# RMSNorm with each row written twice: rows spread in place to eight output rows in one buffer, one 64 KB run per partition and store, all transfers issued by SyncE

## Chip, cores, metric

One core of a Trainium2 chip, the other cores idle. The metric is the device time of one execution in microseconds (us). Most executions of the kernel before agree within 0.2%. A run more than 1.5% above the fastest of its kernel is called slow and left out of every comparison. "MB" is a million bytes. "Kilobytes" of a row or a packet are 1024 bytes.

## The reference

Every row of x is repeated, divided by its root mean square and multiplied by gamma.

```python
B, S, D = 8, 512, 2048                      # x: float32, 4096 rows of 8 KB
x_rep = np.repeat(x, 2, axis=1)             # each row twice, one after the other
rms = np.sqrt((x_rep ** 2).mean(axis=-1, keepdims=True) + 1e-6)
return (x_rep / rms) * gamma[None, None, :] # 8192 rows of 8 KB
```

The kernel must read 33.55 MB and write 67.11 MB. The two copies of a row are neighbours in memory, so the results of k neighbouring rows fill one run of 2k x 8 KB.

## The kernel before

Two rows per partition, 16 tiles, six buffers for x and six for the result. Each tile is loaded by SyncE in one transfer and stored by GpSimd in two, one for each copy.

```python
K = 2
x_t = x_f.rearrange("(n p k) d -> n p k d", p=P, k=K)
out_t = out_v.rearrange("(n p k) r d -> n p k r d", p=P, k=K)
BUFS = 6
# ... pools, gamma: loaded by SyncE, then copied to all partitions by GpSimd ...
for i in range(ntiles):
    x_tile = xin.tile([P, K, D], mybir.dt.float32, name="x_tile")
    nc.sync.dma_start(out=x_tile[:], in_=x_t[i])
    sq_tile = sq.tile([P, K, D], mybir.dt.float32, name="sq_tile")
    # ... ScalarE: Square of each row into sq_tile with the sum in ss; Sqrt; VectorE: reciprocal ...
    y_tile = sq_tile
    for k in range(K):
        nc.vector.tensor_scalar_mul(
            out=y_tile[:, k, :], in0=x_tile[:, k, :], scalar1=rstd[:, k : k + 1])
    nc.vector.tensor_mul(out=y_tile[:], in0=y_tile[:], in1=gamma_kd)
    for r in range(R):
        nc.gpsimd.dma_start(out=out_t[i, :, :, r, :], in_=y_tile[:])
```

Of the kernel before, what the change touches and what calls it, by code (L numbers as in the profile page):

```python
# [1 line left out]

# [4 lines left out]


@with_exitstack  # L10
def kernel(
    ctx: ExitStack,
    tc: tile.TileContext,
    x: bass.AP,
    gamma: bass.AP,
    out: bass.AP,
):
    nc = tc.nc
    P = nc.NUM_PARTITIONS

    B, S, D = x.shape
    Bo, So, Do = out.shape
    R = So // S
    assert D == Do and B == Bo and So == S * R
    eps = 1e-6

    x_f = x.rearrange("b s d -> (b s) d")
    N = B * S
    K = 2
    assert N % (P * K) == 0  # L30
    ntiles = N // (P * K)
    x_t = x_f.rearrange("(n p k) d -> n p k d", p=P, k=K)

    out_v = out.rearrange("b (s r) d -> (b s) r d", r=R)
    out_t = out_v.rearrange("(n p k) r d -> n p k r d", p=P, k=K)

    BUFS = 6
    singles = ctx.enter_context(tc.tile_pool(name="singles", bufs=1))
    xin = ctx.enter_context(tc.tile_pool(name="xin", bufs=BUFS))
    sq = ctx.enter_context(tc.tile_pool(name="sq", bufs=BUFS))  # L40
    small = ctx.enter_context(tc.tile_pool(name="small", bufs=8))

    gamma_b = singles.tile([P, D], mybir.dt.float32)
    nc.sync.dma_start(out=gamma_b[0:1, :], in_=gamma.partition_broadcast(1))
    nc.gpsimd.partition_broadcast(out_ap=gamma_b[:], in_ap=gamma_b[0:1, :])  # L45
    gamma_kd = bass.AP(
        tensor=gamma_b.tensor,
        offset=gamma_b.offset,
        ap=[gamma_b.ap[0], [0, K], gamma_b.ap[1]],
    )  # L50

    eps_t = singles.tile([P, 1], mybir.dt.float32)
    nc.vector.memset(eps_t, eps)  # L53

    inv_d = 1.0 / float(D)

    for i in range(ntiles):
        x_tile = xin.tile([P, K, D], mybir.dt.float32, name="x_tile")
        nc.sync.dma_start(out=x_tile[:], in_=x_t[i])

        sq_tile = sq.tile([P, K, D], mybir.dt.float32, name="sq_tile")
        ss = small.tile([P, K], mybir.dt.float32, name="ss")
        for k in range(K):
            nc.scalar.activation(  # L64
                out=sq_tile[:, k, :],
                in_=x_tile[:, k, :],
                func=mybir.ActivationFunctionType.Square,
                accum_out=ss[:, k : k + 1],
            )

        rms = small.tile([P, K], mybir.dt.float32, name="rms")
        nc.scalar.activation(  # L72
            out=rms[:],
            in_=ss[:],
            func=mybir.ActivationFunctionType.Sqrt,
            scale=inv_d,
            bias=eps_t[:],
        )
        rstd = small.tile([P, K], mybir.dt.float32, name="rstd")
        nc.vector.reciprocal(out=rstd[:], in_=rms[:])  # L80

        y_tile = sq_tile
        for k in range(K):
            nc.vector.tensor_scalar_mul(  # L84
                out=y_tile[:, k, :], in0=x_tile[:, k, :], scalar1=rstd[:, k : k + 1]
            )
        nc.vector.tensor_mul(out=y_tile[:], in0=y_tile[:], in1=gamma_kd)  # L87

        for r in range(R):
            nc.gpsimd.dma_start(out=out_t[i, :, :, r, :], in_=y_tile[:])  # L90


# [1 line left out]
_INS = ['x', 'gamma']  # L94
_OUTS = [((8, 1024, 2048), 'float32')]


# [23 lines left out]
```

## Time and profile before

| | before |
|---|---|
| time, median | 245.0 us |
| span of the profiled run | 243.0 us |
| DMA engines full (16 busy) until | 238.7 us |
| last engine moves its last byte at | 240.6 us |

The two lower rows come from the records of single DMA packets in the trace. They list start, duration, size and queue of each packet, but not its engine; "full" means that 16 packets are open at once. The remaining 2.5 us of the span are completion and the end of the program.

The page of the kernel before: busy time by engine, then the DMA engines in 40 slices of 6.1 us (a 9 means 90% or more), and the packets of each queue.

```profile
span 243.0 us, 320 instructions
DVE 112.7 (46%) x65; ACT 69.5 (29%) x82; POOL 30.2 (12%) x37
...
DMA  6999999999999999999999999999999999999993
GB/s 222 431 431 431 391 433 429 436 417 442 422 431 430 433 422 431 429 427 430 425 430 450 410 426 426 430 425 430 429 425 418 418 417 419 430 417 425 417 426 160
...
q0 software_dynamic: 8704, 67.11, 65.7%
q1 hardware_dynamic: 2306, 33.56, 32.8%
```

No compute engine is busy for half of the span, and the DMA engines are full from the second slice to the last but one. So the kernel is bound by its transfers: time can come only from the rate while the engines are full, from the two edges, or from gaps. q0 is GpSimd's queue: 8192 packets of 8 KB and 512 completions. q1 is SyncE's: 2048 packets of 16 KB.

Windows of the same trace (microseconds from the start; columns are busy time of VectorE, ScalarE and GpSimd with instruction counts, the TensorE clock, the DMA share and the rate). A packet is counted where it starts, so short windows are coarse.

```profile
core 0: us, DVE busy (x) ACT busy (x) POOL busy (x), PEclk, DMA share, GB/s
30.00:130.00 100.00, 54.38 (x31) 28.19 (x33) 14.70 (x16) 1.00 1.01 430
140.00:170.00 30.00, 18.89 (x12) 12.57 (x15) 4.09 (x6) 1.00 1.01 428
175.00:200.00 25.00, 14.45 (x8) 4.24 (x6) 3.40 (x5) 1.00 1.01 422
200.00:235.00 35.00, 0.00 (x0) 0.00 (x0) 0.68 (x1) 1.00 1.01 421
```

From 140 us on there are only stores. They begin at 428 GB/s and drop to 421 after 175 us, with the engines full throughout: a packet that took 309 ns takes about 314.

The two costliest compute groups (line, engine, operation, shapes, count | busy us, mean ns | idle before, and what ended it):

```profile
L64 ACT ACTIVATE sq_tile<-x_tile 128x2048 f32<-128x2048 f32 x32 | 60.8, 1901 | 114.1 <-DMA out_dram<-sq_tile 101.1
L87 DVE TENSOR_TENSOR sq_tile<-sq_tile,gamma_b 128x4096 f32<-128x4096 f32 x16 | 70.8, 4422 | 0.5
```

ScalarE stood idle for 114 us, 101 of them until a store had landed and freed a buffer. Compute waits for DMA, not the reverse.

### The profile page before, as it was taken

The numbers are of one execution on the slowest core, as the hardware profiler recorded it, in microseconds if no ns is written. First come the engines' busy times: TensorE is split into PE (matmuls) and PEld (weight loads), VectorE is DVE, ScalarE is ACT, GpSimd is POOL, SyncE is SP. The second block draws the span as 40 slices with busy tenths as digits, with TensorE's granted clock in tenths as the row PEclk, the third lists the DMA queues.
The fourth block names the chain that finished last, engine by engine and source line by source line (L and its number), as shares of the span: only waits on it lengthen the run. The fifth ranks groups of instructions, "written<-read, shape, count | busy, mean of one in ns | idle before, by whom it ended". The sixth has DMA issues, their size and how long they took to land.

```text
span 243.0 us, 320 instructions
## 1 busy us (share of the span) xinstructions
DVE 112.7 (46%) x65; ACT 69.5 (29%) x82; POOL 30.2 (12%) x37
## 2 busy tenths in 40 slices
DVE  0069999950900049680095709577595600000000
ACT  2598656006000150600615061541624000000000
POOL 4003223411010101110130111111121111000000
DMA  6999999999999999999999999999999999999993
GB/s 222 431 431 431 391 433 429 436 417 442 422 431 430 433 422 431 429 427 430 425 430 450 410 426 426 430 425 430 429 425 418 418 417 419 430 417 425 417 426 160
DMA packets 11012, 100.69 MB, mean 414 GB/s; under 512 B 769, under 2 KB 769, under 8 KB 769
## 3 DMA queue, kind: packets, MB, share of 16 engines
q0 software_dynamic: 8704, 67.11, 65.7%
q1 hardware_dynamic: 2306, 33.56, 32.8%
q14 instruction: 2, 0.02, 0.0%
HBM read 33.56 MB, written 67.11 MB: 414 GB/s over the span
## 4 chain that ended last, share of the span: by engine, by line
DMA 50%; another core or an unknown queue 15%; issue 4%; ACT 3%; DVE 2%; POOL 1%; POOLq 0%; ACTq 0%
DMA out_dram<-sq_tile 50%; ACT sq_tile L64 3%; DVE sq_tile L87 2%; POOL out_dram L90 1%; POOLq L116 0%; ACT rms L72 0%; DVE rstd L80 0%; ACTq L64 0%; POOLq L90 0%
## 5 line engine op out<-in xcount | busy, mean ns | idle before, releaser
L64 ACT ACTIVATE sq_tile<-x_tile 128x2048 f32<-128x2048 f32 x32 | 60.8, 1901 | 114.1 <-DMA out_dram<-sq_tile 101.1
L87 DVE TENSOR_TENSOR sq_tile<-sq_tile,gamma_b 128x4096 f32<-128x4096 f32 x16 | 70.8, 4422 | 0.5
L90 POOL DMA_DIRECT2D out_dram<-sq_tile x32 | 27.7, 867 | 169.3 <-DMA out_dram<-sq_tile 125.6
L84 DVE TENSOR_SCALAR sq_tile<-x_tile,rstd 128x2048 f32<-128x2048 f32 x32 | 40.2, 1298 | 0.5
L80 DVE RECIPROCAL rstd<-rms 128x2 f32<-128x2 f32 x16 | 2.6, 163 | 77.8 <-ACT rms L72 77.8
L64 ACT ACTIVATION_READ_ACCUMULATOR sq_tile<-x_tile 128x1 f32 x32 | 6.0, 186 | 0.0
L72 ACT ACTIVATE rms<-ss,eps_t 128x2 f32<-128x2 f32 x16 | 4.7, 296 | 0.5
L45 POOL PARTITION_BROADCAST gamma_b<-gamma_b x1 | 2.3, 2293 | 2.1 <-DMA gamma_b<-in_gamma_dram 2.1
L64 ACT ACT_TABLE_LOAD x1 | 1.3, 1283 | 0.7 <-PEq L105 0.7
L72 ACT ACT_TABLE_LOAD x1 | 1.3, 1283 | 0.0
L53 DVE MEMSET eps_t<- 128x1 f32 x1 | 0.1, 59 | 0.8 <-PEq L105 0.8
L105 POOL MEMSET const-float32-0.0<- 128x1 f32 x1 | 0.1, 99 | 0.2 <-issue 0.2
L105 POOL MEMSET const-uint8-127<- 128x1 uint8 x1 | 0.1, 103 | 0.0
L105 POOL MEMSET const-bfloat16-1.0<- 128x1 bf16 x1 | 0.1, 102 | 0.0
L105 POOL MEMSET const-float32-1.0<- 128x1 f32 x1 | 0.1, 99 | 0.0
## 6 DMA issues: line engine op xcount, KB each, us to landing
out_dram<-sq_tile POOLq DMA_DIRECT2D x32, 2048.0 KB, 40.7
x_tile<-in_x_dram SPq DMA_DIRECT2D x16, 2048.0 KB, 24.4
gamma_b<-in_gamma_dram SPq DMA_DIRECT2D x1, 8.0 KB
```

What stands on the lines that cost most here:

```text
L45: nc.gpsimd.partition_broadcast(out_ap=gamma_b[:], in_ap=gamma_b[0:1, :])
L53: nc.vector.memset(eps_t, eps)
L64: nc.scalar.activation(out=sq_tile[:, k, :], in_=x_tile[:, k, :], func=mybir.ActivationFunctionType.Square, accum_out=ss[:, k : k + 1],)
L72: nc.scalar.activation(out=rms[:], in_=ss[:], func=mybir.ActivationFunctionType.Sqrt, scale=inv_d, bias=eps_t[:],)
L80: nc.vector.reciprocal(out=rstd[:], in_=rms[:])
L84: nc.vector.tensor_scalar_mul(out=y_tile[:, k, :], in0=x_tile[:, k, :], scalar1=rstd[:, k : k + 1])
L87: nc.vector.tensor_mul(out=y_tile[:], in0=y_tile[:], in1=gamma_kd)
L90: nc.gpsimd.dma_start(out=out_t[i, :, :, r, :], in_=y_tile[:])
L105: nc = _bacc.Bacc("TRN2", target_bir_lowering=False, num_devices=1)
```

## The change

Intent: fewer and longer packets, one queue, no store work on GpSimd. A buffer of 64 KB per partition holds eight output rows. Four rows of x are loaded into its upper half; row after row is normalized into its place and copied to the row beside it (three copies on ScalarE, one on VectorE). The whole buffer is then one store, one run of 64 KB per partition. There are three such buffers and eight tiles; SyncE issues loads and stores. Scale and gamma are fused in one VectorE instruction, and squares go to PSUM, a memory apart from the buffers that the transfers use.

```diff
-    K = 2
+    K = 4
-    xin = ctx.enter_context(tc.tile_pool(name="xin", bufs=BUFS))
-    sq = ctx.enter_context(tc.tile_pool(name="sq", bufs=BUFS))
+    rows = ctx.enter_context(tc.tile_pool(name="rows", bufs=3))
+    junk = ctx.enter_context(tc.tile_pool(name="junk", bufs=1, space=bass.MemoryType.PSUM))
+    def load(i, parts=1):
+        y = rows.tile([P, K * R, D], f32, name="y")
+        step = K // parts
+        for k in range(0, K, step):
+            at = K * (R - 1) + k
+            nc.sync.dma_start(out=y[:, at : at + step, :], in_=x_t[i, :, k : k + step, :])
+        ys.append(y)
-    nc.sync.dma_start(out=gamma_b[0:1, :], in_=gamma.partition_broadcast(1))
+    load(0, parts=K)
+    nc.scalar.dma_start(out=gamma_b[0:1, :], in_=gamma.partition_broadcast(1))
+    load(1)
+    load(2)
     for i in range(ntiles):
         ...                                  # cut: Square, Sqrt, reciprocal per row
-        nc.vector.tensor_mul(out=y_tile[:], in0=y_tile[:], in1=gamma_kd)
-        for r in range(R):
-            nc.gpsimd.dma_start(out=out_t[i, :, :, r, :], in_=y_tile[:])
+            nc.vector.scalar_tensor_tensor(
+                out=y0, in0=xk, scalar=rstd[:], in1=gamma_b[:], op0=Alu.mult, op1=Alu.mult)
+            if k == K - 1:
+                nc.vector.tensor_copy(out=y1, in_=y0)
+            else:
+                nc.scalar.copy(out=y1, in_=y0)
+        nc.sync.dma_start(out=out_t[i], in_=y.rearrange("p j d -> p (j d)"))
+        if i >= 1 and i + 2 < ntiles:
+            load(i + 2)
```

More of the change, by code (lines that the diff above doesn't have):

```diff
@@ L19 @@
     P = nc.NUM_PARTITIONS
+    f32 = mybir.dt.float32
+    Act = mybir.ActivationFunctionType
+    Alu = mybir.AluOpType
     B, S, D = x.shape
@@ L23 @@
     R = So // S
-    assert D == Do and B == Bo and So == S * R
+    assert R == 2 and D == Do and B == Bo and So == S * R
     eps = 1e-6
-    x_f = x.rearrange("b s d -> (b s) d")
+    inv_d = 1.0 / float(D)
+    K = 4
     N = B * S
-    K = 2
     assert N % (P * K) == 0
     ntiles = N // (P * K)
-    x_t = x_f.rearrange("(n p k) d -> n p k d", p=P, k=K)
-    out_v = out.rearrange("b (s r) d -> (b s) r d", r=R)
-    out_t = out_v.rearrange("(n p k) r d -> n p k r d", p=P, k=K)
-    BUFS = 6
+    x_t = x.rearrange("b s d -> (b s) d").rearrange("(n p k) d -> n p k d", p=P, k=K)
@@ L38 @@
+    out_t = out.rearrange("b s d -> (b s) d").rearrange("(n p j) d -> n p (j d)", p=P, j=K * R)
     singles = ctx.enter_context(tc.tile_pool(name="singles", bufs=1))
-    xin = ctx.enter_context(tc.tile_pool(name="xin", bufs=BUFS))
-    sq = ctx.enter_context(tc.tile_pool(name="sq", bufs=BUFS))
+    rows = ctx.enter_context(tc.tile_pool(name="rows", bufs=3))
+    junk = ctx.enter_context(tc.tile_pool(name="junk", bufs=1, space=bass.MemoryType.PSUM))
     small = ctx.enter_context(tc.tile_pool(name="small", bufs=8))
-    gamma_b = singles.tile([P, D], mybir.dt.float32)
@@ L44 @@
-    nc.sync.dma_start(out=gamma_b[0:1, :], in_=gamma.partition_broadcast(1))
-    nc.gpsimd.partition_broadcast(out_ap=gamma_b[:], in_ap=gamma_b[0:1, :])
-    gamma_kd = bass.AP(
-        tensor=gamma_b.tensor,
-        offset=gamma_b.offset,
-        ap=[gamma_b.ap[0], [0, K], gamma_b.ap[1]],
-    )
-    eps_t = singles.tile([P, 1], mybir.dt.float32)
+    ys = []
+    def load(i, parts=1):
[5 more added lines that the diff above has]
+        ys.append(y)
@@ L53 @@
+    load(0, parts=K)
+    gamma_b = singles.tile([P, D], f32, name="gamma_b")
+    nc.scalar.dma_start(out=gamma_b[0:1, :], in_=gamma.partition_broadcast(1))
+    nc.gpsimd.partition_broadcast(out_ap=gamma_b[:], in_ap=gamma_b[0:1, :])
+    eps_t = singles.tile([P, 1], f32, name="eps_t")
     nc.vector.memset(eps_t, eps)
-    inv_d = 1.0 / float(D)
+    load(1)
+    load(2)
     for i in range(ntiles):
-        x_tile = xin.tile([P, K, D], mybir.dt.float32, name="x_tile")
-        nc.sync.dma_start(out=x_tile[:], in_=x_t[i])
-        sq_tile = sq.tile([P, K, D], mybir.dt.float32, name="sq_tile")
-        ss = small.tile([P, K], mybir.dt.float32, name="ss")
+        y = ys[i]
@@ L63 @@
         for k in range(K):
-            nc.scalar.activation(
-                out=sq_tile[:, k, :],
-                in_=x_tile[:, k, :],
-                func=mybir.ActivationFunctionType.Square,
-                accum_out=ss[:, k : k + 1],
-            )
-        rms = small.tile([P, K], mybir.dt.float32, name="rms")
-        nc.scalar.activation(
-            out=rms[:],
-            in_=ss[:],
-            func=mybir.ActivationFunctionType.Sqrt,
-            scale=inv_d,
-            bias=eps_t[:],
-        )
@@ L79 @@
-        rstd = small.tile([P, K], mybir.dt.float32, name="rstd")
-        nc.vector.reciprocal(out=rstd[:], in_=rms[:])
-        y_tile = sq_tile
-        for k in range(K):
-            nc.vector.tensor_scalar_mul(
-                out=y_tile[:, k, :], in0=x_tile[:, k, :], scalar1=rstd[:, k : k + 1]
-            )
-        nc.vector.tensor_mul(out=y_tile[:], in0=y_tile[:], in1=gamma_kd)
-        for r in range(R):
-            nc.gpsimd.dma_start(out=out_t[i, :, :, r, :], in_=y_tile[:])
+            xk = y[:, K * (R - 1) + k, :]
@@ new lines @@
+            y0, y1 = y[:, R * k, :], y[:, R * k + 1, :]
+            sq = junk.tile([P, D], f32, name="sq")
+            ss = small.tile([P, 1], f32, name="ss")
+            nc.scalar.activation(out=sq[:], in_=xk, func=Act.Square, accum_out=ss[:])
+            rms = small.tile([P, 1], f32, name="rms")
+            nc.scalar.activation(out=rms[:], in_=ss[:], func=Act.Sqrt, scale=inv_d, bias=eps_t[:])
+            rstd = small.tile([P, 1], f32, name="rstd")
+            nc.vector.reciprocal(out=rstd[:], in_=rms[:])
@@ L94 @@
+            nc.vector.scalar_tensor_tensor(
+                out=y0, in0=xk, scalar=rstd[:], in1=gamma_b[:],
+                op0=Alu.mult, op1=Alu.mult,
+            )
+            if k == K - 1:
[5 more added lines that the diff above has]
+            load(i + 2)
 _INS = ['x', 'gamma']
```

## The prediction

> **What bounds the kernel now.** The DMA engines. The page's DMA row is at 9 in every slice but the first and last, and 100.69 MB moved at a mean of 414 GB/s. VectorE is busy 46% of the span, ScalarE 29%, GpSimd 12%; the list of waits shows them waiting for stores (101.1 us on ScalarE). From the packet records: a store packet (8 KB, software queue, 8192 of them) takes 309 ns at nearly every percentile; a load packet (16 KB, hardware queue, 2048) takes 611 ns at the median. Over 16 engines that is 158.2 + 78.2 = 236.4 us. By windows of half a microsecond, data flows from about 2.1 us until most engines end near 238.5-239 and the last at about 240.3; the span is 243.0, the time 245.04. Only some 8 us are not DMA-full.
>
> **What the change does.** Bytes stay: 33.6 MB in, 67.1 MB out. The bound moves only through packet size and edges.
> - Packets. Two 8 KB packets take 618 ns, one of 16 KB 611: about 7 ns fixed each, and 302 ns per 8 KB. Estimate: 32 KB takes 1.21 us, 64 KB 2.42 us. Stores 64 x 2.42 = 154.8 us (-3.4); loads 56 x 1.21 + 32 x 0.309 = 77.8 us (-0.4). DMA sum 232.6, a gain of 3.8. The Trainium skill, "DMA: Bandwidth & Descriptors" (Why small descriptors are slow), has such a fixed cost per packet; the size here is from the trace. It gives a fabric ceiling of 435 GB/s, which for 100.66 MB is 231.3 us.
> - Start: x's first load is issued at 0.7 us, not 1.1 behind gamma: -0.4.
> - End: no store descriptors written by GpSimd, perhaps engines that end together: 0 to -0.8.
> - Buffers are 3 and loads queue behind stores. Per tile of four rows, estimates from the trace: ScalarE 4 x 1.95 + 4 x 0.35 + 3 copies at about 1.9 = 15 us; VectorE 4 x (0.17 + 2.2) + one copy at 1.3 = 11 us. From landing to the last copy about 17 us, against a DMA period of 29 us per tile. In steady state a store of 19.4 us is always queued while the next load waits for a buffer: no gap. Only at the end is it tight: the last load lands about 1.7 us after its data, compute takes 17, issue to first byte 1.1, against the 19.4 us of the store before: a gap of 0 to 1 us.
>
> **Critical path.** Compute is off it before and after: GpSimd's 27.7 us of store issue, the fused multiply and ScalarE's copies are worth nothing by themselves.
>
> **Sum.** 245.0 - 3.8 (packets) - 0.4 (start) - 0.6 (end) + 0.4 (last gap) = 240.6 us. Range 239.1 to 243.2. Faster by over 2% (under 240.1) 0.40, within 2% 0.56, slower 0.04.
>
> **What would show it.** One hardware queue; store packets of 64 KB at about 2.42 us (if they are cut to 16 KB, 611 ns and the gain is 2.2); DMA at 9 in all middle slices, 430-434 GB/s; DMA starting at 1.7 us; last store issued at or just after the end of the one before; VectorE busy about 90 us, ScalarE about 120.
>
> **What would make it wrong.** Stores on the hardware queue slower than 27 GB/s per engine, or 64 KB runs conflicting in HBM (time above 243); loads and stores in one queue leaving gaps at each switch; a compute tile longer than about 19 us, which opens a gap at the end and, past 26 us, at each tile.

## The result

The changed kernel takes 240.79 us in the median of four runs (239.93 to 241.71), the kernel before 245.0. Ratios here are the mean time of one kernel's fast runs over that of the other's of the same rounds, so not quite the ratio of the quoted medians: 0.9829, with a 95% interval of 0.9803 to 0.9854. That is 1.7% faster, less than the 2% that would be called faster.

The page after, the same lines:

```profile
span 239.1 us, 293 instructions
DVE 88.8 (37%) x73; ACT 116.3 (49%) x122; POOL 2.5 (1%) x5
...
DMA  7999998989899999899898999899989899898984
GB/s 262 426 454 439 439 439 351 526 351 526 351 428 439 493 395 451 384 411 510 362 515 351 439 439 506 373 422 433 493 384 471 362 461 461 384 482 384 493 384 175
...
q1 hardware_dynamic: 2736, 100.66, 98.3%
```

There is one queue, with a quarter of the packets. The jumping GB/s row (351, then 526) is no stop and go: long packets are counted where they start. Wider windows show the rate:

```profile
core 0: us, DVE busy (x) ACT busy (x) POOL busy (x), PEclk, DMA share, GB/s
40.00:120.00 80.00, 26.45 (x21) 34.18 (x37) 0.00 (x0) 1.00 1.01 435
120.00:200.00 80.00, 28.38 (x23) 34.51 (x37) 0.00 (x0) 1.00 1.00 432
200.00:215.00 15.00, 10.20 (x9) 13.63 (x15) 0.00 (x0) 1.00 0.98 424
215.00:218.00 3.00, 0.91 (x1) 0.00 (x0) 0.00 (x0) 1.00 0.92 393
218.00:235.00 17.00, 0.00 (x0) 0.00 (x0) 0.00 (x0) 1.00 1.00 432
```

The compute groups after:

```profile
L71 ACT ACTIVATE sq<-y 128x2048 f32<-128x2048 f32 x32 | 59.7, 1865 | 92.5 <-DMA y<-in_x_dram 92.5
L76 DVE SCALAR_TENSOR_TENSOR y<-y,rstd,gamma_b 128x2048 f32<-128x2048 f32 x32 | 75.3, 2352 | 1.2
L83 ACT COPY y<-y 128x2048 f32<-128x2048 f32 x24 | 44.7, 1890 | 3.2 <-DVE y L76 3.2
```

ScalarE works 47 us more than before and VectorE 24 us less, as predicted (about 120 and 90 us), and neither matters. The main wait has changed its name: ScalarE now waits for loads (92.5 us), because a load cannot be issued before a whole store has left its buffer.

The packet records give the two numbers on which the predicted gain rested. The rates are for stretches that hold (nearly) only that packet, each packet's bytes spread over its duration:

```
packet     median ns   rate in such a stretch    spacing on one engine (16 x bytes / rate)
  8 KB         309     428.0 GB/s (before, 150-170 us, stores)        306.2 ns
 16 KB         611     431.3 GB/s (before,   8-20 us, loads)          607.8 ns
 32 KB        1213     433.0 GB/s (after,   12-20 us, loads)         1210.8 ns
 64 KB        2418     434.3 GB/s (after,   60-70 us, stores)        2414.4 ns
```

The 64 KB packet came out as estimated (2.42 us). But packets overlap on an engine by 2 to 4 ns, so durations overstate the cost of many packets. By durations a packet costs 7.7 ns beyond its bytes, by spacing 5.0 ns: (8 x 306.2 - 2414.4) / 7.

### The profile page after: what moved, and what is told of

It is laid out like the page before. It is cut to its first block, busy times and chain, and to the rows that moved or that the text cites. A ratio compares the mean times of both kernels' runs of the same rounds, so it can differ in the third digit from the quotient of the medians.

```text
span 239.1 us, 293 instructions
## 1 busy us (share of the span) xinstructions
DVE 88.8 (37%) x73; ACT 116.3 (49%) x122; POOL 2.5 (1%) x5
## 4 chain that ended last, share of the span: by engine, by line
DMA 68%; ACT 13%; DVE 8%; SPq 1%; issue 1%
DMA y<-in_x_dram 41%; DMA out_dram<-y 27%; ACT sq L71 7%; DVE y L76 6%; ACT y L83 5%; DVE y L81 2%; SPq L52 1%; ACT rms L73 1%; DVE rstd L75 0%; SPq L84 0%
## 5 line engine op out<-in xcount | busy, mean ns | idle before, releaser
L71 ACT ACTIVATE sq<-y 128x2048 f32<-128x2048 f32 x32 | 59.7, 1865 | 92.5 <-DMA y<-in_x_dram 92.5
L76 DVE SCALAR_TENSOR_TENSOR y<-y,rstd,gamma_b 128x2048 f32<-128x2048 f32 x32 | 75.3, 2352 | 1.2
L75 DVE RECIPROCAL rstd<-rms 128x1 f32<-128x1 f32 x32 | 5.1, 159 | 124.8 <-ACT rms L73 124.8
L83 ACT COPY y<-y 128x2048 f32<-128x2048 f32 x24 | 44.7, 1890 | 3.2 <-DVE y L76 3.2
L81 DVE COPY y<-y 128x2048 f32<-128x2048 f32 x8 | 9.8, 1226 | 0.3
L73 ACT ACTIVATE rms<-ss,eps_t 128x1 f32<-128x1 f32 x32 | 9.4, 293 | 0.7
L71 ACT ACTIVATION_READ_ACCUMULATOR sq<-y 128x1 f32 x32 | 6.0, 186 | 0.0
```

The source lines that it names most:

```text
L71: nc.scalar.activation(out=sq[:], in_=xk, func=Act.Square, accum_out=ss[:])
L73: nc.scalar.activation(out=rms[:], in_=ss[:], func=Act.Sqrt, scale=inv_d, bias=eps_t[:])
L75: nc.vector.reciprocal(out=rstd[:], in_=rms[:])
L76: nc.vector.scalar_tensor_tensor(out=y0, in0=xk, scalar=rstd[:], in1=gamma_b[:], op0=Alu.mult, op1=Alu.mult,)
L81: nc.vector.tensor_copy(out=y1, in_=y0)
L83: nc.scalar.copy(out=y1, in_=y0)
```

## The experiments

Twelve kernels ran; all gave correct results. Medians below are of fast runs alone. Each trace is of one run only, so what is read from it holds for that run. The changed kernel ran again beside the first three others, as their anchor on the same chip; its ratio there was 0.984 (241.3 us median, 240.22 to 242.02).

> The changed kernel itself, as the anchor of this chip. Expected 240.8 us (239.9 to 241.7), 4.2 us under the kernel before.

### Long packets or another queue: g8, swstore, before_hw

**g8** leaves queue, order, buffers and compute of the changed kernel alone, but puts a gap of 32 bytes after each row of the buffer, so that neither side of a transfer can be cut longer than one row.

```diff
-        y = rows.tile([P, K * R, D], f32, name="y")
+        y = rows.tile([P, K * R, D + 8], f32, name="y")      # rows used as y[:, j, :D]
-        nc.sync.dma_start(out=out_t[i], in_=y.rearrange("p j d -> p (j d)"))
+        nc.sync.dma_start(out=out_t[i].rearrange("p (g e) -> p g e", g=8), in_=y[:, :, :D])
```

> The changed kernel with a gap of 32 bytes after each row of the buffer: same queue, order, buffers and compute, but loads and stores go in packets of 8 KB. Packet theory: 768 packets per engine; by the spacing of 8 KB packets in the trace before (306.4 ns) 235.3 us of DMA against 232.2 after, so 3.1 us slower than the changed kernel (243.9); by the packet durations of the records 4.7 us slower (245.5). Rival, that the gain is the move of the stores from the software to the hardware queue: as the changed kernel, 240.8, and its 8 KB packets do not stretch from 309 to 315 ns late in the span.

Measured: 244.6 us (243.31 to 245.44), ratio 0.9973 to the kernel before. The mean of its runs is 3.3 us above the anchor's of the same chip. The DMA part of its page and its windows:

```profile
DMA packets 12596, 100.69 MB, mean 417 GB/s; under 512 B 305, under 2 KB 305, under 8 KB 305
...
q1 hardware_dynamic: 12592, 100.66, 99.3%
```

```profile
40.00:120.00 80.00, 26.65 (x21) 33.11 (x36) 0.00 (x0) 1.00 1.01 425
120.00:200.00 80.00, 28.38 (x23) 35.17 (x37) 0.00 (x0) 1.00 1.01 425
200.00:235.00 35.00, 11.11 (x9) 14.25 (x15) 0.00 (x0) 1.00 1.01 429
```

All 12288 data packets are 8 KB now, and the rate falls from 432-435 to 425 GB/s with compute untouched. Going from 32 and 64 KB packets to 8 KB costs 3.3 us (about 0.9 either way, by the intervals of the two ratios). The size agrees with spacing (3.1) and not with durations (4.7). It is more than the change itself got from packets, since loads of the kernel before were already in 16 KB: by spacing that is 2.5 of the 4.2 us. Stores in 8 KB packets stay at 429 GB/s to the end here, so the late drop to 421 GB/s in the kernel before is not a matter of packet size alone. It goes with GpSimd's queue: before_hw below has the 8 KB stores of the kernel before on SyncE's queue and holds 428.0 GB/s from 200 to 230 us; before_fused, on GpSimd's, is at 419 from 200 to 235 us; and in spread2, on GpSimd's, a 32 KB packet takes 1220 ns from 200 us on instead of 1213. Why it begins late is open.

**swstore** keeps the 64 KB runs and gives the stores back to GpSimd.

```diff
-        nc.sync.dma_start(out=out_t[i], in_=y.rearrange("p j d -> p (j d)"))
+        nc.gpsimd.dma_start(out=out_t[i], in_=y.rearrange("p j d -> p (j d)"))
```

> The changed kernel with the eight stores issued by GpSimd on the software queue, runs of 64 KB kept. Packet theory: packets of 64 KB at about 2.42 us, the same stream, only the end about 1 us later (a software queue ended 2.5 us before the span's end, the hardware queue 1.45): 241 to 242. Queue rival: back to 244 to 245. If the software queue cuts the runs, the packet records will show it and the test is one of packet size again.

Measured: 243.4 us (one slow run of 253.3 left out), ratio 0.9927: 2.1 us above the anchor (by the two ratios). Both theories missed. Packets on the software queue also took 2418 ns, and by 200 us more had been moved than in the changed kernel (85.15 MB against 84.99). The loss comes in one piece:

```profile
core 0: us, DVE busy (x) ACT busy (x) POOL busy (x), PEclk, DMA share, GB/s
200.00:214.00 14.00, 5.50 (x6) 10.78 (x12) 0.00 (x0) 1.00 0.96 417
214.00:217.00 3.00, 2.96 (x3) 2.57 (x4) 0.00 (x0) 1.00 0.41 175
217.00:221.00 4.00, 2.65 (x2) 0.90 (x1) 0.53 (x1) 1.00 0.04 16
221.00:240.00 19.00, 0.00 (x0) 0.00 (x0) 0.00 (x0) 1.00 1.02 442
```

From about 216 to 221 us the engines are nearly idle while VectorE finishes the last tile; its store is issued at 220.2 us, in the changed kernel at 216.0. In sum each engine idles for 4.8 us between 200 and 222 us. That is more than the 3.5 us by which this run is slower than the changed kernel's; engines that end 0.2 us apart instead of 1.5 gave some back. The last load landed at 203.1 us instead of 199.4, and the packet records show that one engine did this: the other 15 had completed it by 199.7 us. On the last one a load packet took 1.90 us instead of 1.21 and ended at 200.4 us, and a 64 KB store packet had its turn before the completion, until 202.8 us. (The profiled run is the slowest of the fast ones, 244.38 us; whether the others lost their time in the same way was not seen.)

How the two queues share the engines can be counted. Of packets that start between 60 and 100 us, 176 are the loads' 32 KB packets and 176 the stores' 64 KB packets. Chained to 16 engines by their starts and ends, nine of ten neighbours are a load and a store. The Trainium skill, "DMA: Bandwidth & Descriptors" (Queues, rings and completion order), says that an engine alternates between its queues packet by packet; this trace agrees, with one record of 32 or 64 KB as the unit. Two queues share turns, not bytes: the loads got 144 GB/s, the stores 289. Sharing also delays stores: the one that freed the buffer for the last load took 37.6 us from issue to landing instead of 32.0, so that this load was issued at 168.0 us instead of 159.7. In the kernel before it was the other way round: between 40 and 50 us, 175 load packets of 16 KB to 175 store packets of 8 KB, so loads had two thirds, ran ahead and were all done at 135 us.

**before_hw** does the reverse: the kernel before with its stores on SyncE. Six loads are issued ahead, each later load after the stores of the tile whose buffer it takes.

```diff
-            nc.gpsimd.dma_start(out=out_t[i, :, :, r, :], in_=y_tile[:])
+            nc.sync.dma_start(out=out_t[i, :, :, r, :], in_=y_tile[:])
+        if i + BUFS < ntiles:
+            load(i + BUFS)
```

> The kernel before with its stores on SyncE's hardware queue, six loads issued ahead and each later load after the stores of its buffer's tile; packets stay 8 KB and 16 KB. Packet theory: stream unchanged (about 235 us), gain only from the end (1 us) and from the late slow stretch if that belongs to the software queue (1 us): 243 to 244. Queue rival: 241.

Measured: 248.65 us (248.49 to 248.78), ratio 1.0146. Both theories had the sign wrong. The late slow stretch is gone (428.0 GB/s from 200 to 230 us, 421 in the kernel before), as the packet theory allowed, but the end is worse:

```profile
200.00:236.00 36.00, 0.00 (x0) 0.00 (x0) 0.00 (x0) 1.00 1.01 429
236.00:239.00 3.00, 0.00 (x0) 0.00 (x0) 0.00 (x0) 1.00 0.90 382
239.00:241.00 2.00, 0.00 (x0) 0.00 (x0) 0.00 (x0) 1.00 0.31 131
241.00:243.00 2.00, 0.00 (x0) 0.00 (x0) 0.00 (x0) 1.00 0.21 90
243.00:245.00 2.00, 0.00 (x0) 0.00 (x0) 0.00 (x0) 1.00 0.17 74
```

Eleven engines are done by 239.5 us; five are not, and three of these go on beyond 243, the last until 245.3. Engines have drifted apart, and what one loses no other makes up. The records also show packets that take longer than the median of their size; in before_hw they are nearly all loads. In sum per engine, all packets together ran over by:

```
                                       us per engine, at      first idle to
                                    20-36 us   36-170 us   last byte (us)
before       two queues                 0.49        0.06   238.7 -> 240.6
before_fused two queues                 0.41        0.72   239.5 -> 242.5
swstore      two queues                 0.94        0.09   240.7 -> 240.9
spread2      two queues                 0.74        0.80   242.5 -> 242.8
after        one queue,  8 loads/8      1.07        0.47   236.2 -> 237.7
again        one queue,  8 loads/8      0.99        0.65   235.8 -> 237.0
endsplit     one queue,  8 loads/8      1.41        0.29   235.9 -> 237.5
oldstart     one queue,  8 loads/8      0.04        2.30   237.4 -> 238.8
g8           one queue,  8 loads/8      0.50        0.89   239.1 -> 240.1
k2           one queue, 16 loads/16     0.79        0.75   236.2 -> 239.7
before_hw    one queue, 16 loads/32     0.53        1.54   238.6 -> 245.3
before_hw_k  one queue, 16 loads/32     0.32        1.64   238.9 -> 244.4
```

("again" is the anchor; 8 loads/8 means eight tiles loaded and eight stores; the last tile of endsplit is split. The two profiles that fell on slow runs, before_spread and swsplit, are left out.) The sums do not tell one queue from two, nor few changes from many: over both stretches they go from 0.55 to 1.54 us with two queues, and from 1.39 (g8) to 2.34 us (oldstart) with eight loads and eight stores in one. What does go with the number of transfers in one queue is the time from the first idle engine to the last byte: 1.0 to 1.5 us in five traces, then 3.5, then 5.5 and 6.7.

### Is it the changes from store to load: k2, before_hw_k

**k2** is the changed kernel with twice as many, half as large transfers.

```diff
-    K = 4
+    K = 2
-    rows = ctx.enter_context(tc.tile_pool(name="rows", bufs=3))
+    rows = ctx.enter_context(tc.tile_pool(name="rows", bufs=6))
-        if i >= 1 and i + 2 < ntiles:
-            load(i + 2)
+        if i >= 1 and i + 5 < ntiles:          # and loads 1 to 5 ahead of the loop
+            load(i + 5)
```

> The changed kernel with two rows per partition and six buffers: 16 loads in 16 KB packets, 16 stores in 32 KB packets, twice the changes between load and store in the one queue. Packet theory alone: 0.8 us slower than the changed kernel (by 16 KB and 32 KB packet spacings of 608.8 and 1210.8 ns), 241.8. If each change from store to load in one queue costs (as the stretched load packets of the run before_hw suggest), 1.5 to 3 us slower, 242.5 to 244, with engines that end further apart.

Measured: 244.04 us (242.89 to 244.19), ratio 0.9943, 2.5 us above the changed kernel by the ratios (0.984 and 0.9943 of 245.0). Packets explain 0.8 of it. The rest goes with engines that end 3.5 us apart instead of 1.5. This is the size and the end that the second theory expected, but not its mechanism: packets ran over by 1.54 us per engine between 20 and 170 us, just as in the changed kernel.

**before_hw_k** asks whether before_hw suffered from its stores' gaps in HBM (each wrote every other row). Its two stores per tile are cut by row, and each writes both copies of a row, 16 KB in one run.

```diff
-        for r in range(R):
-            nc.sync.dma_start(out=out_t[i, :, :, r, :], in_=y_tile[:])
+        for k in range(K):                     # y_rep: row k, repeated by a step of 0
+            nc.sync.dma_start(out=out_t[i, :, k, :, :], in_=y_rep)
```

> The run before_hw with its two stores per tile cut by row instead of by copy: each writes both copies of one row, 16 KB in one run in HBM, from a repeated source; same queue, number of transfers and of changes from store to load. If before_hw's 3.6 us come from changes between store and load in one queue: still 248 to 249, load packets between 36 and 170 us stretched by 1.5 us per engine in sum, 3 to 5 engines ending 5 us late. If they come from rows written with gaps: 243 to 245.

Measured: 250.41 us (fast runs 247.89 to 251.33; one of 251.84 left out), ratio 1.0194. The gaps in HBM are not the cause, and writing without them was not faster. The same stretched loads and stragglers appear. That stragglers go with more transfers, and so more changes between loads and stores, in one queue holds over the one-queue runs above as a pattern; packet sizes differ with it. What stretches a load, and what makes some engines end late, stays open. No run put the stores on a second hardware queue, so one shared queue and the kind of queue are not told apart here.

### Compute: before_fused

```diff
-            nc.vector.tensor_scalar_mul(...)
-        nc.vector.tensor_mul(out=y_tile[:], in0=y_tile[:], in1=gamma_kd)
+            nc.vector.scalar_tensor_tensor(out=y_tile[:, k, :], in0=x_tile[:, k, :],
+                scalar=rstd[:, k : k + 1], in1=gamma_b[:], op0=mult, op1=mult)
```

> The kernel before with the scale and the multiplication by gamma in one VectorE instruction per row, as in the change; nothing else. Packet theory: VectorE loses 35 of its 113 us and the time does not move, 245.0 within 0.5. Rival, that compute was part of the gain: 1 us or more faster.

Measured: 246.27 us (245.79 to 246.88), ratio 1.004. Less VectorE work gained nothing, so the rival is out. It even lost 1.0 us: packets ran over by 0.72 us per engine between 36 and 170 us (0.06 before), and engines ended 3.0 us apart instead of 1.9. Why was not found.

### Long packets alone in the old kernel: before_spread, spread2

**before_spread** puts both copies of a row into one buffer (three of them, as they are twice as large), so that each tile has one store of 32 KB runs on GpSimd's queue.

```diff
-    sq = ctx.enter_context(tc.tile_pool(name="sq", bufs=BUFS))
+    sq = ctx.enter_context(tc.tile_pool(name="sq", bufs=BUFS // R))    # tiles [P, K, R, D]
-        for r in range(R):
-            nc.gpsimd.dma_start(out=out_t[i, :, :, r, :], in_=y_tile[:])
+        for k in range(K):
+            nc.scalar.copy(out=y_tile[:, k, 1, :], in_=y_tile[:, k, 0, :])
+        nc.gpsimd.dma_start(out=out_t[i].rearrange("p k r d -> p (k r d)"),
+                            in_=y_tile.rearrange("p k r d -> p (k r d)"))
```

> The kernel before with one part of the change alone: both copies of a row in one buffer (ScalarE copies), so that each of its 16 stores, still on the software queue, writes one run of 32 KB per partition. Packet theory: packets of 32 KB, 128 x 1.211 us instead of 512 x 306.4 ns per engine, 1.9 us less, and 1 us more if the slow packets of the last 60 us belong to small packets of the software queue: 242 to 243. Rival, that packets do nothing on the software queue: 245.0.

Measured: 245.6 us, ratio 1.0018 (two slow runs left out; the profile fell on one of them). The experiment was spoilt by my own edit: squares were written into the store buffers, so ScalarE could not start a tile before an old store had landed. **spread2** sends squares to PSUM instead.

```diff
-                out=sq_tile[:, k, 0, :],
+                out=sqj[:],                    # a [P, D] tile in PSUM
```

> The run before_spread mended: squares go to PSUM, not into the store buffers, so that ScalarE no longer waits for a store to land before it squares the next tile; stores of 32 KB runs on the software queue, all else as before. Packet theory: no stretches of idle engines after 180 us, stream at 432 GB/s, 242 to 243. If packets are worth nothing here: 245 with no idle stretches.

Measured: 245.27 us (244.77 to 246.34), ratio 1.0008. Again no gain, against the theory, and again a stretch of idle engines: from 180 to 190 us the stream ran at 272 GB/s, which at 430 is a loss of 3.7 us. The windows, then the chain of waits that led there (start, us, what):

```profile
140.00:178.00 38.00, 17.48 (x10) 20.29 (x19) 1.07 (x2) 1.00 1.00 428
178.00:184.00 6.00, 5.96 (x4) 3.70 (x2) 0.53 (x1) 1.00 0.32 137
184.00:190.00 6.00, 5.96 (x4) 3.70 (x2) 0.35 (x1) 1.00 0.86 366
```

```profile
121.83 18.34 DMA x_tile<-in_x_dram
...
151.48 0.02 SPq L60
151.50 0.03 issue
151.53 18.33 DMA x_tile<-in_x_dram
...
178.77 2.40 DVE sq_tile L86 x2
181.17 0.02 issue
181.19 1.60 DVE sq_tile L89
```

The chain runs through loads of 2 MB that take 18.3 us. Their last packet ends at 168 us, in the kernel before at 135. While both queues had work, packets alternated nearly one to one here too (99 loads to 80 stores between 140 and 150 us), but a turn of the stores is now 32 KB. So loads fell behind, and the stores ran dry before the last tiles were computed. On this reading longer store packets paid for themselves and then lost it to slowed loads. The profiled run took 246.34 us, the longest of the six; without the 3.7 us it would be about 242.6, inside the expected 242 to 243. That is an argument, not a run: there are also three store buffers here instead of six of half the size, and their part was not separated.

### The ends: swsplit, oldstart, endsplit

**swsplit** tried to close swstore's gap: the last tile alone is loaded row by row and stored in two halves.

```diff
-            load(i + 2)
+            load(i + 2, parts=K if i + 2 == ntiles - 1 else 1)
+            if i == ntiles - 1 and k % 2 == 1:   # store four output rows; whole stores for other tiles
+                nc.gpsimd.dma_start(out=out_t[i][:, 4*h*D : 4*(h+1)*D], in_=...)   # h = k // 2
```

> The changed kernel with stores on the software queue as in the run swstore, and the last tile alone loaded in four rows and stored in two halves. If the 4.5 us by which the stream of swstore stood still after 215 us is a wait of the last store for the last tile's compute (its load now shares the engines with the store before and lands later), the gap goes and the time is 239.5 to 240.5. If the gap is a property of the software queue, 243.6 as swstore.

Measured: 246.32 us (fast runs 245.71 to 247.44), ratio 1.006, worse than swstore by about 3 us. My edit was wrong, in a way that fits the shares: the row loads come in 8 KB packets, and each of these, it seems, now waits a turn of a 64 KB store packet. The last row was issued at about 173 us and landed at 222.5. That profile fell on a slow run, so only the sign is used, which the fast runs share.

**endsplit** is the same edit in the changed kernel, where the one queue was served in order: in its trace the load issued at 159.7 us has its packets from 187.4 us on, after those of the store issued at 156.9 us.

> The changed kernel with the last tile alone loaded in four rows and stored in two halves, all in the one SyncE queue, so that its last store need not wait for the whole tile. In the trace after the last store was issued about when the one before it ended, with a gap of 0.2 us: expected gain 0 to 0.4 us, 240.6 to 241.0. If the compute of the last tile costs more than seen, up to 1 us. The 8 KB loads do not starve as in the run swsplit[...].

Measured: 240.51 us (239.69 to 241.29), ratio 0.9814 against the 0.9829 and 0.984 of the changed kernel. It is the fastest median of all, but the difference of 0.4 to 0.6 us is within the scatter. It does show that row loads do no harm without a second queue beside them.

**oldstart** gives the changed kernel the old start.

```diff
-    load(0, parts=K)
-    nc.scalar.dma_start(out=gamma_b[0:1, :], in_=gamma.partition_broadcast(1))
+    nc.sync.dma_start(out=gamma_b[0:1, :], in_=gamma.partition_broadcast(1))
+    load(0)                                     # after gamma's broadcast, ahead of load(1)
```

> The changed kernel with the start of the kernel before: gamma first on SyncE, then the first tile in one load. Predicted term of the start 0.4 us; the bytes delivered by 5 us put it at 0.7 (1.13 MB against 0.83). Expected: 0.83 MB by 5 us, 0.7 us slower, 241.7, within the scatter of the changed kernel's runs (239.9 to 242.0), so the bytes decide and not the time. Rival, that the start gives nothing: 1.13 MB by 5 us.

Measured: 241.57 us (241.35 to 241.9), ratio 0.9858. By 5 us 0.95 MB had been moved, against 1.13 after and 0.83 before. So the expected 0.83 was missed. The 0.18 MB are 0.4 us of stream at 433 GB/s, the size that the prediction gave to the start. The time can't show it: packets of this run also ran over by more (2.34 us per engine between 20 and 170 us, 1.54 in the changed kernel).

## Why the prediction was right

The time came within 0.2 us of the forecast, partly by compensation. Its sum against what the traces show:

| term | predicted | measured | from |
|---|---|---|---|
| packets, by size | -3.8 | -2.5 | spacings of the packet table: stores 512 x 306.2 ns to 64 x 2414.4 (-2.3), loads -0.2 |
| slow stores after 175 us | none | -1.0 | 63 us at 421 instead of 428 GB/s before; absent after |
| start | -0.4 | -0.7 | 1.13 against 0.83 MB by 5 us |
| last byte to end of span | -0.6 (both end terms: no store issue on GpSimd, engines that end together) | -1.1 | 2.5 us before, 1.4 after; 1.7 in swstore, whose stores are GpSimd's |
| engines ending apart | (in the line above) | -0.4 | 1.9 us before, 1.5 after |
| last gap | +0.4 | +0.2 | engines idle between 215 and 220 us, in sum |
| stretched loads | none | +1.0 | 20 to 36 us: 0.49 to 1.07; 36 to 170 us: 0.06 to 0.47 |

The measured column is read from the two traces; runs isolate only packets (g8) and start (oldstart). It adds up to -4.5; the spans differ by 4.0, so half a microsecond is not placed.

- **"DMA bound, compute off the path": right.** before_fused took work from VectorE without gain, and the changed kernel gave ScalarE 47 us more without loss.
- **Packets: the mechanism right, the size off.** g8 undid packet size alone (loads even below their 16 KB before) and lost 3.3 us. "302 ns per 8 KB" plus "about 7 ns fixed each" took the durations in the records as if packets followed each other end to end. They overlap by a few nanoseconds, so 3.8 should have been 2.5. The Trainium skill, "DMA: Bandwidth & Descriptors" (Where 436 GB/s comes from), puts the ceiling at 435 GB/s. The changed kernel runs at up to 434.3, so next to nothing is left in packets.
- **End and start: right in sign, too small.** 2.2 us against 1.0 (of the start's 0.7, oldstart isolates 0.4). The pieces were read from windows that count a packet where it starts.
- **Missing on both sides.** The late slow stores of the kernel before were in the windows and not seen (a gain of 1.0). Loads that stretched more than before were not foreseen either (a loss of 1.0). That this is the price of one queue is not shown: over the same two stretches spread2 with two queues has 1.54 us, as the changed kernel has. Gain and loss happen to cancel, which is luck.
- **The last gap: right.** The last store was issued at 216.0 us, about when the one before it ended.
- **What was not asked: why one queue.** The prediction gave the queue only the end; the late slow stores (1.0 us) went with GpSimd's queue too. With long store packets on a second queue, spread2's chain ran through slowed loads, and in swstore one engine's late load packet held back the last tile; before_hw shows that one queue with many small transfers is worse than two. The change works as a whole: long packets, few transfers, one order. Which part one order has was not isolated.

## What to carry to other kernels

When two DMA queues both have work, compare their packet sizes: they took turns by packet here, so the longer packets get the larger share, and lengthening the stores slows the loads. Take a packet's cost from the spacing of packets in a full stretch, not from the duration of one, and look at when the first and the last engine end. Here, with the DMA engines already full, packets of 32 and 64 KB instead of 8 KB were worth about 1.3% (3.3 of 244 us), and freeing a compute engine bought nothing.

## What the Trainium skill lacked or had wrong

- "DMA: Bandwidth & Descriptors", Queues, rings and completion order: it gives turns by packet, with a packet of several descriptors. Here the turn was one run of up to 64 KB (176 to 176 packets of 32 and 64 KB), and the consequence is lacking: loads had 144 GB/s beside 289 for stores.
- The same page, Rules for kernel authors, says that spreading transfers over issuing engines does nothing for bandwidth. The rate agrees (about 433 GB/s in swstore as in the changed kernel). But the split changed when transfers landed (the last load at 203.1 instead of 199.4 us), and swstore was 2.1 us slower.
- The same page, Issuing engine by pattern, calls the hardware queues generally faster. Moving the old kernel's stores to the hardware queue that its loads use made it slower by 1.5% (248.65 against 245.0 us), with five engines ending up to 6.7 us late; a hardware queue of their own was not tried. No page that I read has this drift of engines in one mixed queue.
- The same page, Where 436 GB/s comes from, lets HBM bind at about 358 GB/s per core. The page's own note on its measurements gives that rate for both cores of a pair at work, and for one core alone its table has more. The trace agrees with the note: with one core working, up to 434 GB/s were sustained.
- The same page, Why small descriptors are slow, gives the fixed cost of a packet in cycles, worked out for 256 bytes only. Here a packet cost 5.0 ns beyond its bytes, and going from 8 KB to 32 and 64 KB still gave 3.3 us of 244 (g8).
